# Two-layer hybrid diffusion block: layer 1's modulation weights over GpSimd's queue, the state-space convolutions started earlier, one mLSTM query tile placed in front of a norm

## The chip, the cores and the metric

The kernel runs on one core of one Trainium2 chip. The metric is device time in microseconds of that core, the median of three runs. Below, PE is TensorE, DVE is VectorE, ACT is ScalarE, POOL is GpSimd and SP is SyncE. Nearly all loads are issued on SP's DMA queue.

## The reference, cut to what matters

Two layers run over 256 latent tokens and 256 context tokens of width 1024. The modulation vectors of each layer come from a small product with a wide weight, `w_mod[l]`, of 1024 x 6144; its twelve 512-column chunks are shift, scale and gate of the mixers (chunks 0 to 5) and of the MLP (6 to 11).

```python
for l in range(DEPTH):
    mod_l = silu(c) @ w_mod[l] + b_mod[l]          # and the same with c_ctx for the context
    h = LN(x) * (1 + scale_a) + shift_a            # both streams
    p = split(h @ w_in[l])                         # four mixers:
    a = diff_attention(...)                        # A differential attention
    b = mlstm(silu(dwconv(qk, 5 taps)), ...)       # B
    m = latent_attention(rms_norm(cq) @ w_uq, ...) # C (called mla in the kernel)
    s = ssd(silu(dwconv(xbc, 5 taps)), ...)        # D state space
    y = (sum_k sigmoid(h @ w_gate[k] + b_gate[k]) * (branch_k @ w_branch[k])) @ w_o[l]
    x = LN(alpha * x + gate_a * y)
    u = relu(h2 @ w_up + b_up); x = LN(alpha * x + gate_m * (u * u @ w_down + b_down))
```

In the last layer only the latent stream's output is needed.

## The kernel before, in words

**Products.** Each fp32 product is made of three TensorE products of parts rounded to float32r. `load` (from L154) takes a weight tile of 128 x 1024 (512 KB) over SP's queue into one of four `raw` tiles (L167); ACT writes the high part `whi` (L169), DVE the low part `wlo` (L170), three tiles of each; `three` (L181 to L183) issues the three matmuls. A tile of eight 128 x 128 blocks feeds 24 matmuls.

**Order.** Each engine executes its own list of instructions strictly in the order in which the program's scheduler has put them. The program itself interleaves work by hand: `along(quantum, generator)` starts a side generator that gets one step for every so many microseconds of planned TensorE time of the main line, and `finish` runs what is left of it. `load` takes one step of a list `bg` whenever it is called, as long as the list has any.

**One layer.** `mixers` first makes the mLSTM tile 0 (`mlstm_in`, 24 matmuls a tile in layer 0), the latent attention's compressed queries (`mla_cq`: per token tile a square with a sum on ACT, L1179, a power on POOL, L245, a scaled copy on ACT, L1181, and three transposes on PE, L237 out of `D`), then `mla_in`, and then runs gates and latent attention beside the remaining mLSTM and state-space input tiles. `mlstm_conv` and `ssd_conv` are the five-tap convolutions on DVE (`conv`: L642 four times a tile and L645), six tiles of them for the state space. `merge` makes gated sums of the branches, with the mLSTM, its output and the state-space recurrence running beside it; the mLSTM's own steps on DVE are L678 (a masked bank that PE fills at L660) and L792.

**Modulation of layer 1.** It is computed during layer 0's MLP, chunks 1 and 2 of its four chunks of 1024 hidden units, by 32 `bg` steps. `mod_steps` (chunks 0 to 3) loads four `T` tiles of 128 x 512 on SP's queue (L392) for each of the eight 128-row blocks and multiplies them on PE (L408). `mod_slow` (chunks 4 to 11) loads one `T` tile of 256 KB a step on SP's queue (L434), one ahead within a chunk, and multiplies it on DVE by one column of `ct` (L446 the first, L448 the others: 64 in all). `T` is a pool of eight tiles. `br` is a pool of three larger tiles, two of which hold `x`. In `down`, DVE adds finished banks into `acc` at L1517 and so frees the banks for PE; POOL's queue brings bias rows into `acc` (L1511) and gate rows into `T` (L1485).

Of the kernel before, what the change touches and what calls it, by code (L numbers as in the profile page):

```python
# [10 lines left out]
F32 = mybir.dt.float32  # L11
F32R = mybir.dt.float32r
AF = mybir.ActivationFunctionType
# [5 lines left out]
P = 128  # L19
D = 1024  # L20
KT = D // P
# [38 lines left out]
class Kern:  # L60
# [80 lines left out]
    def step(self, g):  # L141
        try:
            next(g[0])
        except StopIteration:
            self.side.remove(g)
# [231 lines left out]
    def mod_steps(self, l, chunks, bank, tile=None, ahead=False):  # L377

        nc = self.nc
        st = {}  # L380

        def fetch(k):
            raws = []
            for a in range(0, len(chunks), 2):
                if tile is None:
                    raw = self.raw.tile([P, 1024], F32, tag="raw", name="raw")
                    raws += [raw[:, 0:512], raw[:, 512:1024]]
                    nc.sync.dma_start(raw, self.ap["w_mod"][l, k * P:(k + 1) * P, chunks[a] * 512:chunks[a] * 512 + 1024])
                else:
                    for i in range(2):  # L390
                        raws.append(tile())
                        nc.sync.dma_start(raws[-1], self.ap["w_mod"][l, k * P:(k + 1) * P, chunks[a + i] * 512:chunks[a + i] * 512 + 512])  # L392
            st[k] = raws

        def step(k):
            if not ahead:
                fetch(k)
            elif k < KT:
                fetch(k)
                k -= 1  # L400
                if k < 0:
                    return
            else:
                k -= 1
            if k == 0:
                st["ps"] = bank()
            for j in range(len(chunks)):
                nc.tensor.matmul(st["ps"][32 * j:32 * j + 32, :], self.ct[:, k, :], st[k][j],  # L408
                                 start=k == 0, stop=k == KT - 1, tile_position=(0, 32 * j))
            if k == KT - 1 and not ahead:  # L410
                finish()

        def finish():
            n = 32 * len(chunks)
            sb = self.dt_()
            nc.scalar.activation(sb[0:n, :], st["ps"][0:n, :], AF.Copy)
            pt = self.mx()
            for b in range(4):
                self.tr(pt[:, b * P:b * P + n], sb[0:n, b * P:(b + 1) * P])
            for j, ch in enumerate(chunks):  # L420
                self.mod_finish(l, ch, pt.rearrange("p (b r) -> p b r", r=P)[:, :, 32 * j:32 * j + 2], slice(0, 2))

        if ahead:
            return [lambda k=k: step(k) for k in range(KT + 1)] + [finish]
        return [lambda k=k: step(k) for k in range(KT)]

    def mod_slow(self, l, ch, streams):

        nc = self.nc
        acc, ws = {}, {}  # L430

        def fetch(k):
            ws[k] = self.tmp()
            nc.sync.dma_start(ws[k], self.ap["w_mod"][l, k * P:(k + 1) * P, ch * 512:(ch + 1) * 512])  # L434

        def step(k):
            if k == 0:
                fetch(0)
            if k + 1 < KT:
                fetch(k + 1)  # L440
            w = ws.pop(k)
            for s in streams:
                cv = self.ct[:, k, s:s + 1]
                if k == 0:
                    acc[s] = self.tmp()
                    nc.vector.tensor_scalar(acc[s], w, cv, None, op0=ALU.mult)  # L446
                else:
                    nc.vector.scalar_tensor_tensor(acc[s], w, cv, acc[s], op0=ALU.mult, op1=ALU.add)  # L448
            if k == KT - 1:
                pt = self.mx()  # L450
                for s in streams:
                    for b in range(4):
                        o = 8 * s + 2 * b
                        nc.tensor.matmul(pt[:, o:o + 2], acc[s][:, b * P:(b + 1) * P], self.ones, start=True, stop=True)
                for s in streams:
                    self.mod_finish(l, ch, pt[:, 8 * s:8 * s + 8].rearrange("p (b r) -> p b r", r=2)[:, :, 0:1], slice(s, s + 1))

        return [lambda k=k: step(k) for k in range(KT)]

    def mod_finish(self, l, ch, src, s):  # L460
        nc = self.nc
# [941 lines left out]
    def mixers(self, l, js, late):  # L1403
        c = slice(js[0] * P, T)
        res = {}
        lat = l == L - 1
        if not lat:
            for f in self.misc0:
                f()
            self.mlstm_in(l, js, (0,))  # L1410
            self.mla_cq(l, js)
            self.mla_in(l, js)
        else:
            self.mla_cq(l, js)
            self.mlstm_o(l, js)
            late()
            self.mlstm_in(l, js, (0,))
            for f in self.misc(l):
                f()
            self.mlstm_in(l, js, (1,))  # L1420
            self.mla_in(l, js)

        ga = self.along(5.0, self.gates(l))
        mla = self.along(2.4 if not lat else 3.0, self.mla(l, js, res))
        self.mlstm_in(l, js, (1, 2, 3) if not lat else (2, 3))
        self.xbc = []
        for i in range(5):
            self.ssd_in(l, js, i)
        self.finish(ga)
        self.finish(mla)  # L1430
        self.mlstm_conv(l, js)
        self.ssd_in(l, js, 5)
        self.mlstm_v(l, js)

        self.acc = [self.accp.tile([P, 512], F32, tag="acc%d" % m, name="acc") for m in range(KT)]
        self.mg = []
        if not lat:
            mods = self.along(8.5, self.bg_gen(self.mod_steps(0, (4, 5, 6, 7), self.ops, ahead=True)
                                               + self.mod_steps(0, (8, 9, 10, 11), self.ops, ahead=True)))
        sc = self.along(8.0 if not lat else 5.0, self.ssd_conv(l, js))  # L1440
        ml = self.along(3.2 if not lat else 2.6, self.mlstm(l, js))
        self.merge(l, 2, res["C"], c, True)
        self.finish(ml)
        if not lat:
            self.mlstm_o(l, js)
        mo = self.along(3.8, self.mlstm_out(l, js, res))
        self.diff_v(l, js)
        self.finish(mo)

        self.finish(sc)  # L1450
        sd = self.along(3.9 if not lat else 2.6, self.ssd(l, js))
        self.diff_k(l, js)
        self.merge(l, 1, res["B"], c)
        self.finish(sd)
        if not lat:
            self.finish(mods)
        self.ssd_z(l, js)
        so = self.along(3.0, self.ssd_out(l, js, res))
        self.diff_q(l, js)
        self.finish(so)  # L1460

        self.dn = {}
        df = self.along(3.3 if not lat else 3.0, self.diff(l, js[-2:] + js[:-2]))
        self.merge(l, 3, res["D"], c)
        self.finish(df)
# [53 lines left out]
    def layer(self, l, late):  # L1519
        nc = self.nc  # L1520
        streams = [1, 0] if l < L - 1 else [1]
        js = [0, 1, 2, 3] if l < L - 1 else [2, 3]
# [8 lines left out]
        def out_proj(s):  # L1531
            g = self.gate_row(l, 0, s)
            sums = self.residual(self.ap["w_o"][l], self.mg, x, toks(s), g)
            st = self.ln_stats([x(t) for t in toks(s)], toks(s), sums)
            return {t: self.ln_again(x(t), self.ln_affine(x(t), st[t], g1)) for t in toks(s)}
# [5 lines left out]
        for i, s in enumerate(streams):  # L1541
# [4 lines left out]
            st = out_proj(s)  # L1546
# [5 lines left out]
        self.acc = [None] * KT  # L1552

        if l + 1 < L:
            a = self.mod_steps(l + 1, (0, 1, 2, 3), self.mx, self.tmp)
            b = sum((self.mod_slow(l + 1, ch, (1,)) for ch in range(4, 12)), [])
            bg = sum(([*a[i // 4:i // 4 + (i % 4 == 0)], *b[2 * i:2 * i + 2]] for i in range(32)), [])
            n = len(bg)
        for ch in range(3):
            us = []  # L1560
# [12 lines left out]
        for i, s in enumerate(streams):  # L1573
# [9 lines left out]
            st = {}  # L1583
            for t in toks(s):
# [4 lines left out]
                else:  # L1589
                    for i in range(2):  # L1590
                        c = slice(i * 512, (i + 1) * 512)
# [145 lines left out]
```

## Time and profile before

| | |
|---|---|
| median of 3 runs | 1835.34 us (1834.81 to 1838.74) |
| profiled execution | 1835.2 us |
| its span in the profile | 1833.4 us (1.8 us lie around it) |
| PE busy | 1757.4 us, 96% |
| DVE busy | 1195.0 us, 65% |
| ACT busy | 865.7 us, 47% |
| POOL busy | 81.3 us, 4% |
| moved from HBM | 264.75 MB |
| mean granted TensorE clock | 0.982 of full speed |

An engine's share is its busy time over the span of the profiled execution. A line number names the line of the kernel that issued an instruction; `out<-in` names its tiles. In brackets stands how long the engine was idle before an instruction, and the instruction that released it.

### The profile page before, as it was taken

Reading aid. Unit: us, or ns where it says so; the run is one execution under the profiler, and the core shown is the slowest. Engines: PE = TensorE matmul, PEld = TensorE weight load, DVE = VectorE, ACT = ScalarE, POOL = GpSimd, SP = SyncE. Lnnn points to the kernel's source line nnn. Section 1 sums busy time; section 2 is a strip of 40 time slices with the busy share of each in tenths; the row PEclk is TensorE's granted clock in tenths of the full one; section 3 lists DMA queues with packets and bytes.
Section 4 is the critical chain, followed back from the end, with each engine's and each line's share of the span. In section 5 each row is a group of like instructions: output and inputs, shape, how many; then the busy total and the mean of one; then the engine's idle time right before and its main releaser. Section 6 shows DMA issues by size and latency. Waiting matters only on the chain.

```text
span 1833.4 us, 27817 instructions
## 1 busy us (share of the span) xinstructions
PE 1757.4 (96%) x10612; PEld 1489.0 (81%) x10612; DVE 1195.0 (65%) x2324; ACT 865.7 (47%) x1655; POOL 81.3 (4%) x119
## 2 busy tenths in 40 slices
PE   6889999999999999999999999899999999979997
PEld 3777877877887799888777798877989988969996
DVE  4566476355557668885656469867485777676666
ACT  3545354245435545664313246654364555545552
POOL 0100000000000001100000001110000000000000
PEclk9999999999999999999999999899999999989998
DMA  8131244543231256786776656431233353646653
GB/s 326 51 103 41 76 133 138 144 150 127 74 116 64 81 184 187 238 271 210 196 216 219 164 158 205 150 103 55 93 104 93 104 172 115 208 151 194 185 186 100
DMA packets 86981, 269.73 MB, mean 147 GB/s; under 512 B 10368, under 2 KB 11392, under 8 KB 86848
## 3 DMA queue, kind: packets, MB, share of 16 engines
q1 hardware_dynamic: 83056, 256.14, 45.0%
q0 software_dynamic: 3792, 11.82, 2.1%
q8 instruction: 83, 1.36, 0.3%
q14 instruction: 50, 0.41, 0.1%
HBM read 264.75 MB, written 3.17 MB: 146 GB/s over the span
## 4 chain that ended last, share of the span: by engine, by line
PE 84%; DVE 7%; issue 3%; ACT 3%; DMA 2%; POOL 1%; SPq 0%; POOLq 0%; DVEq 0%; ACTq 0%
PE mm L181 18%; PE mm L182 17%; PE mm L183 17%; PE O L181 3%; PE O L183 3%; PE O L182 3%; PE mx L237 3%; PE mx L181 3%; PE mx L183 3%; PE mx L182 3%; DMA T<-w_mod 2%; PE O L1112 2%; DVE wlo L170 1%; PE mx L1145 1%; ACT whi L169 1%
## 5 line engine op out<-in xcount | busy, mean ns | idle before, releaser
L170 DVE TENSOR_TENSOR wlo<-raw,whi 128x1024 fp32r<-128x1024 f32 (+3 forms) x388 | 461.6, 1190 | 329.6 <-ACT whi L169 325.6
L169 ACT ACTIVATE whi<-raw 128x1024 fp32r<-128x1024 f32 (+3 forms) x388 | 400.7, 1033 | 545.1 <-PE mm L182 196.1
L181 PE MATMUL mm<-h,whi 128*128 128x256 f32 (+1 forms) x1216 | 418.4, 344 | 1.1 <-ACT D L1310 1.1
L183 PE MATMUL mm<-h,wlo 128*128 128x256 f32 (+1 forms) x1216 | 408.9, 336 | 1.0 <-DVE wlo L170 1.0
L182 PE MATMUL mm<-h,whi 128*128 128x256 f32 (+1 forms) x1216 | 408.5, 336 | 0.0
L181 PEld LDWEIGHTS mm<-h,whi 128*128 128x128 f32 x1216 | 232.1, 191 | 46.2 <-issue 19.4
L183 PEld LDWEIGHTS mm<-h,wlo 128*128 128x128 f32 x1216 | 231.8, 191 | 25.5 <-DVE wlo L170 1.7
L182 PEld LDWEIGHTS mm<-h,whi 128*128 128x128 f32 x1216 | 232.0, 191 | 22.1 <-issue 1.9
L181 PE MATMUL mm<-whi,L 128*128 128x512 f32 (+1 forms) x344 | 134.0, 390 | 4.9 <-DVE acc L1517 3.5
L183 PE MATMUL mm<-whi,L 128*128 128x512 f32 (+1 forms) x344 | 132.6, 386 | 0.0
L182 PE MATMUL mm<-wlo,L 128*128 128x512 f32 (+1 forms) x344 | 132.6, 386 | 0.0
L245 POOL TENSOR_TENSOR s<-s,mhalf 128x1 f32<-128x1 f32 (+2 forms) x52 | 45.5, 876 | 1263.8 <-DVE s L244 1194.5
L181 PEld LDWEIGHTS mm<-whi,L 128*128 128x128 f32 x344 | 64.9, 189 | 22.9 <-issue 5.2
L183 PEld LDWEIGHTS mm<-whi,L 128*128 128x128 f32 x344 | 65.0, 189 | 13.6
L182 PEld LDWEIGHTS mm<-wlo,L 128*128 128x128 f32 x344 | 65.1, 189 | 12.9
L237 PE MATMUL mx<-kc,T 128*128 128x128 f32 x320 | 52.5, 289 | 23.4 <-DVE T L283 13.8
L1096 ACT ACTIVATE T<-mx,s 128x512 f32<-128x512 f32 (+1 forms) x72 | 44.1, 615 | 64.9 <-DVE s L1094 64.8
L181 PE MATMUL mm<-whi,h 128*128 128x256 f32 x256 | 73.2, 288 | 0.7 <-ACT whi L169 0.5
L182 PE MATMUL mm<-wlo,h 128*128 128x256 f32 x256 | 72.2, 283 | 0.0
L183 PE MATMUL mm<-whi,h 128*128 128x256 f32 x256 | 71.6, 283 | 0.0
L237 PEld LDWEIGHTS mx<-kc,T 128*128 128x128 f32 x320 | 39.6, 147 | 36.6 <-DVE T L283 16.0
L181 PE MATMUL O<-h,whi 128*128 128x256 f32 (+1 forms) x224 | 69.1, 308 | 0.0
(341 smaller groups left out, 3475.7 us busy)
## 6 DMA issues: line engine op xcount, KB each, us to landing
raw<-w_up SPq DMA_DIRECT2D x80, 512.0 KB, 3.7
raw<-w_down SPq DMA_DIRECT2D x80, 512.0 KB, 4.2
raw<-w_gate SPq DMA_DIRECT2D x72, 512.0 KB, 3.6
raw<-w_in_fm SPq DMA_DIRECT2D x52, 512.0 KB, 3.6
T<-w_mod SPq DMA_DIRECT2D x96, 256.0 KB, 3.9
raw<-w_branch SPq DMA_DIRECT2D x36, 512.0 KB, 3.7
raw<-w_mod SPq DMA_DIRECT2D x32, 512.0 KB, 3.7
raw<-w_o SPq DMA_DIRECT2D x24, 512.0 KB, 4.4
```

The costliest lines, as they stand in the source:

```text
L169: nc.scalar.activation(hi[:, :n], raw[:, :n], AF.Copy)
L170: nc.vector.tensor_sub(lo[:, :n], raw[:, :n], hi[:, :n].bitcast(F32))
L181: mm(ps, a[0], b[0], start=first, stop=False)
L182: mm(ps, a[0], b[1], start=False, stop=False)
L183: mm(ps, a[1], b[0], start=False, stop=last)
L237: self.nc.tensor.transpose(out, in_, self.ident[: in_.shape[0], : in_.shape[0]])
L245: nc.gpsimd.tensor_tensor(out, t, self.mhalf[:, 0:1].to_broadcast([P, n]), op=ALU.pow)
L1096: nc.scalar.activation(Pm[:, 0:nk], S[:, 0:nk], AF.Exp, bias=nm, accum_out=ssum)
L1112: self.nc.tensor.matmul(out, aT[:, b * P:(b + 1) * P], v[b][:, h * P:(h + 1) * P], start=b == 0, stop=b == nb - 1)
L1145: nc.tensor.matmul(S[cc][:, 0:nk], self.dq[h][r, c], self.dk[h][r, 0:nk], start=True, stop=True)
```

## The change

Three parts.

1. Layer 1's modulation weights are loaded by POOL's queue. For chunks 0 to 3, `mod_beside` loads one `br` tile of 1 MB for each block of 128 rows (L436 of the changed kernel) and multiplies it one step later (L431). For chunks 4 to 11, `mod_slow` loads its `T` tiles on POOL's queue (L452), two ahead and across the chunks' borders.
2. `ssd_conv` starts right after `mlstm_conv`, with a quantum of 8.0 in layer 0 and 4.0 in layer 1, instead of at the first merge with 8.0 and 5.0.
3. In layer 0, mLSTM tile 1 stands between `mla_cq` and `mla_in`, instead of behind `mla_in` beside the latent attention.

```diff
+    def mod_beside(self, l, chunks):
...
+        def step(k):
+            if k > 0:
+                if k == 1:
+                    st["ps"] = self.mx()
+                for j in range(4):
+                    nc.tensor.matmul(st["ps"][32 * j:32 * j + 32, :], self.ct[:, k - 1, :], st["w"][:, j, :],
+                                     start=k == 1, stop=k == KT, tile_position=(0, 32 * j))
+            if k < KT:
+                st["w"] = self.br(F32)
+                c = chunks[0] * 512
+                nc.gpsimd.dma_start(st["w"], self.ap["w_mod"][l, k * P:(k + 1) * P, c:c + 2048].rearrange("p (a e) -> p a e", a=4))
+            else:
+                self.mod_turn(l, chunks, st["ps"])
...
-    def mod_slow(self, l, ch, streams):
+    def mod_slow(self, l, chunks, streams):
...
-            nc.sync.dma_start(ws[k], self.ap["w_mod"][l, k * P:(k + 1) * P, ch * 512:(ch + 1) * 512])
...
+        units = [(ch, k) for ch in chunks for k in range(KT)]
...
+        def fetch(i):
+            if i < len(units):
+                ch, k = units[i]
+                ws[i] = self.tmp()
+                nc.gpsimd.dma_start(ws[i], self.ap["w_mod"][l, k * P:(k + 1) * P, ch * 512:(ch + 1) * 512])
...
+        def step(i):
+            ch, k = units[i]
+            if i == 0:
                 fetch(0)
...
+                fetch(1)
+            fetch(i + 2)
+            w = ws.pop(i)
...
             self.mla_cq(l, js)
+            self.mlstm_in(l, js, (1,))
             self.mla_in(l, js)
...
-        self.mlstm_in(l, js, (1, 2, 3) if not lat else (2, 3))
+        self.mlstm_in(l, js, (2, 3))
...
         self.mlstm_conv(l, js)
+        sc = self.along(8.0 if not lat else 4.0, self.ssd_conv(l, js))
         self.ssd_in(l, js, 5)
         self.mlstm_v(l, js)
...
-        sc = self.along(8.0 if not lat else 5.0, self.ssd_conv(l, js))
...
-            a = self.mod_steps(l + 1, (0, 1, 2, 3), self.mx, self.tmp)
-            b = sum((self.mod_slow(l + 1, ch, (1,)) for ch in range(4, 12)), [])
-            bg = sum(([*a[i // 4:i // 4 + (i % 4 == 0)], *b[2 * i:2 * i + 2]] for i in range(32)), [])
+            a = self.mod_beside(l + 1, (0, 1, 2, 3))
+            b = self.mod_slow(l + 1, range(4, 12), (1,))
+            at = {round(31 * i / KT): i for i in range(KT + 1)}
+            bg = sum(([*([a[at[i]]] if i in at else []), *b[2 * i:2 * i + 2]] for i in range(32)), [])
```

What the scheduler made of it is seen in the engines' lists, in three places. The first is PE in layer 0, where `mla_cq` ends; its transposes are the L237 out of `D`, and the L181 to L183 into `mm` are the matmuls of mLSTM tile 1:

```order
 L183 MATMUL mx<-whi,h 128x384
-L237 MATMUL mx<-kc,D 128x128 x10
+L181 MATMUL mm<-h,whi 128x512
+L182 MATMUL mm<-h,whi 128x512
+L237 MATMUL mx<-kc,D 128x128 x3
+L183 MATMUL mm<-h,wlo 128x512
+L181 MATMUL mm<-h,whi 128x512
+L182 MATMUL mm<-h,whi 128x512
+L237 MATMUL mx<-kc,D 128x128 x3
...
+L237 MATMUL mx<-kc,D 128x128
 L237 MATMUL mx<-kc,L 128x128 x8
```

Of the 24 matmuls of mLSTM tile 1, 2 now stand ahead of the first group of three transposes, 3 ahead of the second, 6 ahead of the third, 7 ahead of the fourth, and the last 6 behind them. In exchange 24 matmuls are gone from the stretch of the latent attention: between its last scores and their first transposes stand 6 matmuls and 2 attention products now, where 9 matmuls stood.

The second place is DVE's list in layer 1's first merge, beside the mLSTM (L678 of before is L707 of the changed kernel, L1315 is L1344, L768 is L797). Before:

```order
L642 SCALAR_TENSOR_TENSOR D_12701<-L_12016,cols_118,D_12701 128x2x254
L170 TENSOR_TENSOR wlo_12763<-raw_12761,whi_12762 128x1024
L642 SCALAR_TENSOR_TENSOR D_12701<-L_12016,cols_118,D_12701 128x2x255
L678 SCALAR_TENSOR_TENSOR T_12718<-mx_12715,kc_116 128x256
L642 SCALAR_TENSOR_TENSOR D_12701<-L_12016,cols_118,D_12701 128x2x255
L170 TENSOR_TENSOR wlo_12874<-raw_12872,whi_12873 128x1024
L642 SCALAR_TENSOR_TENSOR D_12701<-L_12016,cols_118,D_12701 128x2x254
L678 SCALAR_TENSOR_TENSOR T_12719<-mx_12715,kc_116 128x256
```

After:

```order
L170 TENSOR_TENSOR wlo_12742<-raw_12740,whi_12741 128x1024
L707 SCALAR_TENSOR_TENSOR T_12697<-mx_12694,kc_116 128x256
L707 SCALAR_TENSOR_TENSOR T_12698<-mx_12694,kc_116 128x256
L797 TENSOR_TENSOR T_12697<-T_12705,T_12697 128x256
L1344 SCALAR_TENSOR_TENSOR acc_12486<-D_12724,mm_12726 128x256
L170 TENSOR_TENSOR wlo_12844<-raw_12842,whi_12843 128x1024
```

The convolutions' steps (L642; L671 of the changed kernel) stand here no more: all of them stand further ahead now, between weight tiles of the mLSTM's values and of the first merge's beginning.

The third place is POOL's list in layer 0's MLP. The rows with L436 and L452 were not on this queue; the L1541 are bias rows of `acc`, the L503 and L1515 gate rows:

```order
+L436 DMA br<-w_mod 128x2048
+L1541 DMA acc<-bdown 128x512
 L245 TENSOR_TENSOR s_7263<-s_7264,mhalf 128x1
 L245 TENSOR_TENSOR s_7269<-s_7270,mhalf 128x1
 L245 TENSOR_TENSOR s_7289<-s_7290,mhalf 128x1
 L245 TENSOR_TENSOR s_7309<-s_7310,mhalf 128x1
...
+L452 DMA T<-w_mod 128x512 x44
+L503 DMA gd_557<-modt_115 128x4x1
+L452 DMA T<-w_mod 128x512 x4
+L436 DMA br<-w_mod 128x2048
```

The loads stand behind the powers of the second stream's norm, 44 in a row. On DVE the 64 multiplies move with them: 34 now stand ahead of the first weight tile of the MLP's chunk 1, where 8 stood. From SP's list 80 rows are gone, among them all loads of layer 1's modulation weights.

## Rows read from the trace of the kernel before

**Rows 1.** The page: busy time and share of the engines, and the chain by engine.

```profile
PE 1757.4 (96%) x10612; PEld 1489.0 (81%) x10612; DVE 1195.0 (65%) x2324; ACT 865.7 (47%) x1655; POOL 81.3 (4%) x119
...
PE 84%; DVE 7%; issue 3%; ACT 3%; DMA 2%; POOL 1%; SPq 0%; POOLq 0%; DVEq 0%; ACTq 0%
```

**Rows 2.** Windows: stretch, its length, PE busy (instructions), granted clock, DMA share, GB/s.

```profile
77.70:84.20 6.50, 2.00 (x12) 0.89 0.29 81
84.20:89.70 5.50, 5.46 (x21) 0.51 0.01 3
933.60:938.00 4.40, 1.05 (x9) 1.00 0.67 206
938.00:943.00 5.00, 4.85 (x14) 0.66 0.93 305
1336.00:1338.10 2.10, 0.81 (x4) 1.00 0.39 92
1338.10:1342.40 4.30, 4.30 (x23) 0.60 0.20 80
```

**Rows 3.** Timeline of PE behind the compressed queries: start, length, instruction [idle before, releaser].

```profile
78.59 0.55 PE L237 MATMUL mx<-kc,D 128*128 128x128 f32 x3 [0.54 <-ACT D L1181]
...
81.82 0.55 PE L237 MATMUL mx<-kc,D 128*128 128x128 f32 x3 [1.69 <-ACT D L1181]
84.24 0.47 PE L237 MATMUL mx<-kc,D 128*128 128x128 f32 x1 [1.88 <-ACT D L1181]
```

**Rows 4.** Timeline of PE in layer 0's MLP, columns as in rows 3.

```profile
938.15 0.47 PE L181 MATMUL mm<-whi,L 128*128 128x512 f32 x1 [3.50 <-DVE acc L1517]
...
938.92 0.39 PE L181 MATMUL O<-whi,L 128*128 128x512 f32 x1
939.15 0.40 PE L182 MATMUL O<-wlo,L 128*128 128x512 f32 x1
```

**Rows 5.** Timeline of DVE ahead of it, columns as in rows 3.

```profile
931.47 0.76 DVE L448 SCALAR_TENSOR_TENSOR T<-T,ct 128x512 f32<-128x512 f32 x1 [1.62 <-DMA T<-w_mod]
...
935.52 0.75 DVE L448 SCALAR_TENSOR_TENSOR T<-T,ct 128x512 f32<-128x512 f32 x1 [1.70 <-DMA T<-w_mod]
...
937.32 0.68 DVE L1517 TENSOR_TENSOR acc<-acc,mm 128x512 f32<-128x512 f32 x1
```

**Rows 6.** Waits of SP's queue: total us, times, longest.

```profile
SPq L434 <- DMA T<-w_mod: 46.5, 27, 7.7
```

**Rows 7.** Timelines of DVE and PE in layer 1's first merge, columns as in rows 3.

```profile
1336.18 0.74 DVE L642 SCALAR_TENSOR_TENSOR D<-L,cols,D 128x508 f32<-128x508 f32 x1
...
1337.41 0.36 PE L660 MATMUL mx<-rhl,e 128*128 128x256 f32 x1 [0.98 <-DVE T L678]
1338.07 0.39 PE L181 MATMUL mm<-h,whi 128*128 128x256 f32 x1 [0.30 <-ACT D L1310]
...
1356.54 0.71 PE L781 MATMUL mx<-st,L 64*128 64x129 f32 x4 [0.98 <-DVE T L792]
```

**Rows 8.** Windows: length, busy of PE, PEld, DVE, ACT, POOL, clock, DMA share, GB/s.

```profile
0.00:46.00 46.00, 31.97 (x140) 16.64 (x140) 20.72 (x76) 15.96 (x30) 3.79 (x12) 0.93 0.88 325
166.00:200.00 34.00, 33.80 (x201) 28.64 (x200) 14.21 (x25) 14.15 (x24) 0.00 (x0) 1.00 0.21 63
800.00:828.00 28.00, 28.00 (x171) 24.97 (x171) 24.43 (x36) 15.75 (x25) 0.00 (x0) 1.00 0.89 291
796.00:861.00 65.00, 64.65 (x378) 56.90 (x378) 47.46 (x67) 35.34 (x52) 0.00 (x0) 1.00 0.75 243
1312.00:1334.00 22.00, 22.00 (x203) 20.97 (x202) 15.74 (x29) 10.34 (x19) 0.00 (x0) 1.00 0.30 97
```

**Rows 9.** Timeline of POOL in layer 0's MLP, columns as in rows 3.

```profile
739.36 0.58 POOL L1511 DMA_DIRECT2D acc<-bdown  x1
...
774.92 2.40 POOL L245 TENSOR_TENSOR s<-s,mhalf 128x1 f32<-128x1 f32 x1 [26.18 <-DVE s L244]
```

More of the change, by code (lines that the diff above doesn't have):

```diff
@@ L413, in finish @@
         def finish():
[L414 to L421, printed above, removed]
+            self.mod_turn(l, chunks, st["ps"])
         if ahead:
@@ L425, in mod_steps @@
         return [lambda k=k: step(k) for k in range(KT)]
-    def mod_slow(self, l, ch, streams):
+    def mod_beside(self, l, chunks):
+        nc = self.nc
+        st = {}
+        def step(k):
[10 more added lines that the diff above has]
+            else:
+                self.mod_turn(l, chunks, st["ps"])
+        return [lambda k=k: step(k) for k in range(KT + 1)]
+    def mod_slow(self, l, chunks, streams):
         nc = self.nc
         acc, ws = {}, {}
-        def fetch(k):
-            ws[k] = self.tmp()
-            nc.sync.dma_start(ws[k], self.ap["w_mod"][l, k * P:(k + 1) * P, ch * 512:(ch + 1) * 512])
-        def step(k):
-            if k == 0:
+        units = [(ch, k) for ch in chunks for k in range(KT)]
[7 more added lines that the diff above has]
+            if i == 0:
                 fetch(0)
-            if k + 1 < KT:
-                fetch(k + 1)
-            w = ws.pop(k)
+                fetch(1)
+            fetch(i + 2)
+            w = ws.pop(i)
             for s in streams:
@@ L456, in step, with mod_turn @@
                     self.mod_finish(l, ch, pt[:, 8 * s:8 * s + 8].rearrange("p (b r) -> p b r", r=2)[:, :, 0:1], slice(s, s + 1))
-        return [lambda k=k: step(k) for k in range(KT)]
+        return [lambda i=i: step(i) for i in range(len(units))]
+    def mod_turn(self, l, chunks, ps):
+        n = 32 * len(chunks)
+        sb = self.dt_()
+        self.nc.scalar.activation(sb[0:n, :], ps[0:n, :], AF.Copy)
+        pt = self.mx()
+        for b in range(4):
+            self.tr(pt[:, b * P:b * P + n], sb[0:n, b * P:(b + 1) * P])
+        for j, ch in enumerate(chunks):
+            self.mod_finish(l, ch, pt.rearrange("p (b r) -> p b r", r=P)[:, :, 32 * j:32 * j + 2], slice(0, 2))
     def mod_finish(self, l, ch, src, s):
```

## The prediction

> **What bounds the kernel now.** I read the page first: PE is busy for 1757.4 of 1833.4 us and holds 84% of the chain that ended last, DVE 7% [rows 1]. So PE is the bound, and the change adds and removes nearly no matmuls. What can be won is PE's idle time, 1833.4 − 1757.4 = 76 us in all, and busy time in which PE's granted clock is low. Then I listed PE's waits and looked for those that stand where the diff touches the order; the windows around each give PE's busy time and the clock. There are three such places, and the reader should see the same pattern in each [rows 2]: a stretch in which PE waits (2.00 us busy of 6.50, 1.05 of 4.40, 0.81 of 2.10), and behind it a stretch in which PE is busy at a clock of 0.51, 0.66 and 0.60 of full speed, between its levels 2.4 and 1.2 GHz. The wait is paid twice.
>
> **Place A, mLSTM tile 1 in front of the norm (layer 0, 78 to 90 us).** The transposes of the compressed queries wait for ACT's scaled copies, with 0.54, 1.69 and 1.88 us of idle time in three of four groups [rows 3]; the chain is ACT, DVE, POOL and ACT again, a token tile at a time, and it does not get shorter. The change puts 18 of the tile's 24 matmuls between these groups. A 512-column matmul takes 0.23 us at full clock (938.92 to 939.15, [rows 4]), so 18 × 0.23 = 4.1 us of work is done while the chain runs, and the group at 84.24 starts when it did. These 4.1 us are then missing later. PE's busy time in the 6.5 us becomes 2.0 + 4.1 = 6.1, so I expect no fall of the clock behind it. That stretch held 5.46 us of work at 0.51 [rows 2]; at full clock it would take 5.46 × 0.51 = 2.8, which is 2.7 less; I take 2.5, since parts of it start by the chain's pace. A gives 6.6. Bounds: 4.1 (the clock falls all the same) and 6.8. The tile's own weight parts cost nothing: their ACT and DVE instructions stand ahead of the chain in the order, where both engines idle.
>
> **Place D, what the tile leaves behind (layer 0, up to 178 us).** In the latent attention the tile's 24 matmuls were cover for softmax. PE lost 0.2 us of 34 in 166 to 200 [rows 8], so there is no wait now. With less cover the whole row of products ends earlier, and between the last scores and their transposes stand 6 matmuls (1.4 us) and two attention products instead of 9 (2.1 us). So at the last few tiles perhaps 0.4 us each comes uncovered: about 1.1 in all for three. Bounds: 0, and 5.5 if all the cover was needed (24 × 0.23). I take 1.1, since the previous stretch has no wait at all.
>
> **Place B, modulation loads off SP (layer 0's MLP, 931 to 943 us).** PE waits 3.50 us for DVE's addition into acc [rows 4], which frees the bank. DVE is late because multiplies of `mod_slow` ahead of it on DVE wait for their `T` tile, 1.62 and 1.70 us at 931.47 and 935.52; the addition comes at 937.32 [rows 5]. The tile is late since its load sits on SP's queue, one ahead only, and the queue itself stood 46.5 us waiting for such tiles [rows 6]. After the change the loads stand on POOL's queue, which has little else, two ahead; and more than half of the multiplies are over before. The wait goes: 3.5 us. The stretch behind it had 4.85 us of work at 0.66 [rows 2], so up to 4.85 × 0.34 = 1.6 comes back, of which I take 1.5. B gives 5.0. Bounds 3.5 and 5.1.
>
> **Place F, where these multiplies go (796 to 861 us).** 34 multiplies instead of 8 now stand on DVE ahead of chunk 1's first weight tile. One takes 0.75 us [rows 5], so 26 × 0.75 = 19.5 us come to the 47.46 us that DVE is busy there in 65 [rows 8]: 67 us. DVE becomes the bound of this stretch by 2 us. The transfers become tight as well: 243 GB/s × 65 us = 15.8 MB; 15 loads of layer 1's modulation go from it (8 for DVE, 7 for PE, 0.26 MB each), 34 come: 20.8 MB. At 325 GB/s, the highest that a window shows, this takes 64 us, and at 291 GB/s, which 800 to 828 had at a share of 0.89, 71.5 us [rows 8]. Two weight tiles that are ready ahead can take up some of it. I take a cost of 3, near DVE's excess plus a little for the transfers. Bounds: 0, and 8 (71.5 − 65 plus something for the excess). Behind it, DVE is freer by the same 19.5 us, but PE has no wait there other than place B.
>
> **The loads' queue.** A load issued by POOL held it for 0.58 us [rows 9], so 34 take 20 us of the 65, and no power or bias row that PE needs soon stands behind them in the order; cost 0. The eight 1 MB tiles have about 22 us of PE work between them, and a tile of that size at 243 GB/s takes 4.3 us; cost 0.
>
> The Trainium skill speaks against this part of the change: by "SBUF — State Buffer" (section "SBUF: two separate sides"), a DMA from GpSimd's queue has its descriptors written by GpSimd, which is locked out while VectorE runs in a mode with two ports, and it advises the SP or ACT queue. Its figure is about 620 ns alone against 3100 ns beside a copy on VectorE; by that, as an estimate, 34 loads would take 105 us instead of 21 and the sum would be some 40 us higher. The trace has the 0.58 us beside a DVE that was busy in most of that time, and agrees with the first figure; no run here shows the second.
>
> **Place C, the convolutions (layer 1, 1336 to 1357 us).** PE waits 0.98 for L678 and 0.30 behind that; DVE had a convolution step of 0.74 us at 1336.18 directly ahead of this L678, and one of the same length ahead of the L792 for which PE waits 0.98 at 1356.54 [rows 7]. After the change no convolution stands there. I count 1.28, 0.7 of the second wait, and the clock: 4.30 us at 0.60 [rows 2] give up to 4.30 × 0.40 = 1.7, of which 1.5. C gives 3.5. Bounds 1.3 and 3.7. What moves ahead, 16 steps of 0.74 = 11.8 us with the closing ones on top, falls into about 1288 to 1330; in 1312 to 1334 DVE was busy for 15.74 of 22 [rows 8], part of which is these same steps, and PE did not wait at all. Cost 0, with 3 as the bound where one step meets a weight tile at the wrong moment several times. In layer 0 the convolutions go from a stretch without waits to 166 to 200, where DVE is busy for 14.21 of 34 [rows 8]: neither gain nor cost.
>
> **The sum**, from the profiled execution's 1835.2 (which is the median, 1835.34, within 0.2): −6.6 (A) − 5.0 (B) − 3.5 (C) + 1.1 (D) + 3.0 (F) = −11.0, so **1824.2 us**.
>
> **Rivals.**
> 1. *The tile was needed as cover* (place D at its bound): 5.5 instead of 1.1, so 1828.6. Against it: PE has no waits there, and 6 matmuls remain between.
> 2. *Stretch F becomes bound by DVE and transfers*: 8 instead of 3, so 1829.2; with the clock falling there too, some 1831. For it: 67 of 65 us on DVE and a rate at the highest seen. Against it: tiles ready ahead, and the multiplies can slip between the `wlo` only if these are late.
> 3. *POOL's queue issues too slowly* (the slower side). One power on POOL took 2.40 us [rows 9]. If a load took that beside a busy DVE, 34 loads would need 82 us in a stretch of 65: the weight tiles of chunk 1 stand behind multiplies that wait, PE loses 17 us, and the time is 1824.2 + 17 = 1841. It decides from 65/34 = 1.9 us a load. Against it: 0.58 [rows 9]. It is the form that the rule quoted above would take here.
> 4. *The waits stay*: the banks in B or the masked bank in C are late for another reason, or the clock stays low. With the lower bounds of A, B and C, 1835.2 − 8.9 + 4.1 = 1830.4. That the change does not do what it says is excluded by the order: the matmuls, loads and steps did move.
>
> **Chances.** The forecast (1819 to 1828) 0.58; rival 1 0.09; rival 2 0.15; rival 3 0.06; rival 4 0.12. About 0.2%, 3.7 us, is what a measurement of this kernel can tell from no change: faster is below 1831.6, slower above 1839. All of the forecast and rival 1, and most of rivals 2 and 4, lie in faster: 0.79. Rival 2 with more lost and rival 4 with D or F at its bound lie within: 0.13. Rival 3, and F and D at their bounds together (1835.2 − 8.9 + 13.5 = 1839.8), are slower: 0.08. The range: all gains at their upper bounds without any cost would give 1835.2 − 15.6 = 1819.6, and it reaches up to where rivals 1, 2 and most of 4 end: 1818 to 1833.
>
> **What would show it.** A: the transposes behind the compressed queries with idle time below 1.3 us together, and a clock near 1 in the 6 us behind. B: no wait of PE for the addition into acc near the end of chunk 2, no load of `w_mod` for layer 1 on SP. C: no idle time of PE ahead of L689 (the old L660) in the first merge, and a clock of 1. D: idle time of PE of some tenths ahead of the last transposes of the latent attention. F: DVE near 100% and 290 to 325 GB/s in the 65 us ahead of chunk 1, with PE waits on `wlo` of about 3 us. The prediction is wrong if PE waits more than 8 us in F, if POOL's DMA issues take over 1.9 us, or if the attention's softmax now ends the waits for over 5 us.

## The result, and the profile after

The changed kernel takes 1825.74 us (median of 6 runs, 1824.92 to 1829.35) against 1836.81 for the kernel before in the same session (6 runs, 1834.81 to 1838.74): a ratio of 0.9943, with a 95% interval of 0.993 to 0.9955. The prediction was 1824.2, range 1818 to 1833. The profiled span goes from 1833.4 to 1824.4 us; that is 9.0 us where the medians differ by 11.1, since the profiled execution of before (1835.2) was shorter than its median.

The page of the changed kernel, busy time and share of the engines, and the chain that ended last, as in [rows 1]:

```profile
PE 1751.1 (96%) x10612; PEld 1482.2 (81%) x10612; DVE 1196.8 (66%) x2324; ACT 866.6 (48%) x1655; POOL 119.2 (7%) x191
...
PE 82%; DVE 7%; issue 5%; ACT 3%; POOL 2%; DMA 1%; SPq 0%; POOLq 0%; ACTq 0%; DVEq 0%
```

POOL has 38 us more: 72 more DMA issues of about half a microsecond. PE has as many matmuls as before and 6.3 us less busy time; the low clock at the places below is the part of it that can be pointed at.

To see where 9.0 us went I walked both traces along PE: each matmul counts as work of the spacing that its shape usually has, and at equal work I took the difference of the two times. Where A ends and D begins, the tile's 24 matmuls lie on different sides of the line in the two kernels, so this walk can't part A from D; A is taken by two instructions instead that both kernels have (the rows under A). The parts of the difference, after minus before, by the places of the prediction:

| stretch | difference, us | forecast |
|---|---|---|
| up to the compressed queries | −0.4 | 0 |
| A: compressed queries and the norm | −4.7 | −6.6 |
| D: attention and its tail | −1.0 | +1.1 |
| the rest of layer 0's mixers, first part of its MLP | +0.2 | 0 |
| F: ahead of chunk 1 | +4.7 | +3.0 |
| B: chunks 1 and 2 up to the old wait | −4.5 | −5.0 |
| from there to layer 1's first merge | +0.1 | 0 |
| C: layer 1's first merge | −4.3 | −3.5 |
| all behind it | +1.0 | 0 |
| sum | −9.0 | −11.0 |

**A.** Windows of PE in the changed kernel (length, PE busy, clock, DMA share, GB/s), to be held against the first two of [rows 2]:

```profile
77.20:83.80 6.60, 6.03 (x30) 1.00 0.12 32
83.80:89.30 5.50, 4.06 (x24) 1.00 0.09 21
```

and its waits of PE from 76 to 93 us (total, times, longest):

```profile
PE mm L181 <- ACT L L1238: 1.4, 1, 1.4
PE mm L181 <- ACT L L1260: 1.0, 1, 1.0
PE mx L237 <- ACT D L1210: 0.5, 2, 0.3
```

PE is busy for 6.03 of 6.60 us where it was for 2.00 of 6.50, the transposes wait for 0.5 us in place of the idle times in [rows 3], and the clock stays at 1.00 where it was 0.51. What this is worth is read from PE's first and last common instruction of the stretch, before and after:

```profile
77.72 0.34 PE L183 MATMUL mx<-whi,h 128*128 128x384 f32 x1
92.43 0.39 PE L181 MATMUL mm<-whi,L 128*128 128x256 f32 x1 [1.01 <-ACT L L1231]
```

```profile
77.29 0.33 PE L183 MATMUL mx<-whi,h 128*128 128x384 f32 x1
83.81 0.33 PE L237 MATMUL mx<-kc,D 128*128 128x128 f32 x1 [0.25 <-ACT D L1210]
92.83 0.39 PE L181 MATMUL mm<-whi,L 128*128 128x256 f32 x1 [1.01 <-ACT L L1260]
```

The way from the first to the last is 14.71 us before and 15.54 after, and the second holds the tile's 24 matmuls more, 24 × 0.23 = 5.5 us of work: A is −4.7. The fourth group of transposes comes 6.52 us behind the first row in both kernels (84.24, in [rows 3], less 77.72; 83.81 less 77.29), so the 18 matmuls ahead of it, 4.1 us, are all gained. Behind it only 0.6 us is.

In the list of waits the first line is new: PE waits 1.4 us for ACT's scaled copy L1238. ACT's timeline shows what stands ahead of it:

```profile
86.43 0.63 ACT L169 ACTIVATE whi<-raw 128x512 fp32r<-128x512 f32 x1
...
87.22 0.59 ACT L718 ACTIVATE L<-mm 128x512 f32<-128x512 f32 x1
87.69 0.69 ACT L1238 ACTIVATE L<-mx,cols 128x512 fp32r<-128x512 f32 x1
```

L718 is the copy of the mLSTM tile's own result. The tile was put in front of the norm with its copy, and that copy now stands ahead of the copy that the next products need. It holds ACT for 0.47 us (87.22 to 87.69). The weight part ahead of it holds ACT for about as long, and it comes late too: in the kernel before, the third weight part of this stretch stands among the transposes.

```profile
78.44 0.62 ACT L169 ACTIVATE whi<-raw 128x512 fp32r<-128x512 f32 x1
```

I take it that the tile's own weights hold one of the three `whi` tiles until its last matmul. Both are a part of the 1.4 us; no run takes either away.

**F and B.** Windows of all engines (columns as in [rows 8]) and PE's clock behind the wait:

```profile
796.00:861.00 65.00, 62.07 (x353) 53.93 (x352) 58.12 (x86) 30.70 (x42) 16.16 (x31) 0.97 0.91 308
```

```profile
845.30:848.30 3.00, 0.41 (x2) 1.00 0.69 232
848.30:853.20 4.90, 4.90 (x15) 0.65 0.88 285
```

The timelines of DVE and PE at the same place:

```profile
844.44 0.75 DVE L467 SCALAR_TENSOR_TENSOR T<-T,ct 128x512 f32<-128x512 f32 x1 [2.15 <-DMA T<-w_mod]
845.76 0.75 DVE L467 SCALAR_TENSOR_TENSOR T<-T,ct 128x512 f32<-128x512 f32 x1 [0.57 <-DMA T<-w_mod]
...
847.57 0.68 DVE L1547 TENSOR_TENSOR acc<-acc,mm 128x512 f32<-128x512 f32 x1
...
848.30 0.50 PE L181 MATMUL mm<-whi,L 128*128 128x512 f32 x1 [2.59 <-DVE acc L1547]
```

This is the picture of [rows 4] and [rows 5] at another place: a multiply waits for its tile, the addition that frees the bank stands behind it, PE waits, and the clock falls behind that. What the change removes near 934 us it makes anew at 845. DVE was busy for 58.12 of 65 us, not for all of it, and it waits for transfers while 308 GB/s flow. POOL's load of the tile for which the multiply at 844.44 waits:

```profile
838.34 0.54 POOL L452 DMA_DIRECT2D T<-w_mod  x1 [2.93 <-DVE T L467]
```

It was issued when a multiply had freed its buffer, and the tile came some 6 us later; the median from issue to landing of the `T` loads of `w_mod` was 3.9 us in the kernel before and is 4.8 in this one. Near 932 us 0.5 us of the old 3.5 is left.

**C.** PE in layer 1's first merge:

```profile
1320.00:1350.00 30.00, 30.00 (x247) 1.00 0.34 112
```

No idle time and no low clock are left of [rows 7] and of the last two of [rows 2]. One wait is new, just ahead of this window:

```profile
1317.64 0.48 DVE L671 SCALAR_TENSOR_TENSOR D<-L,cols,D 128x254 f32<-128x254 f32 x1
...
1318.21 0.42 ACT L673 ACTIVATE D<-D 128x256 f32<-128x256 f32 x1 [0.67 <-DVE D L671]
1318.54 0.46 ACT L1339 ACTIVATE D<-mm,hb 128x256 f32<-128x256 f32 x1
...
1319.05 0.38 PE L181 MATMUL mm<-h,whi 128*128 128x256 f32 x1 [1.05 <-ACT D L1339]
```

The convolutions' own ACT step (L673) waits for their step on DVE and stands ahead of the copy (L1339) for which PE waits. The kernels without the moved convolutions have no wait of PE between 1290 and 1330 us.

### The profile page after: what moved, and what is told of

The parts are those of the page before. It is cut to its first block, busy times and chain, and to the rows that moved or that the text cites. A ratio compares the mean times of both kernels' runs of the same rounds, so it can differ in the third digit from the quotient of the medians.

```text
span 1824.4 us, 27827 instructions
## 1 busy us (share of the span) xinstructions
PE 1751.1 (96%) x10612; PEld 1482.2 (81%) x10612; DVE 1196.8 (66%) x2324; ACT 866.6 (48%) x1655; POOL 119.2 (7%) x191
## 4 chain that ended last, share of the span: by engine, by line
PE 82%; DVE 7%; issue 5%; ACT 3%; POOL 2%; DMA 1%; SPq 0%; POOLq 0%; ACTq 0%; DVEq 0%
PE mm L181 17%; PE mm L183 16%; PE mm L182 16%; PE mx L181 3%; PE mx L183 3%; PE mx L182 3%; PE O L181 3%; PE O L182 3%; PE O L183 3%; PE mx L237 3%; PE O L1141 2%; DVE wlo L170 1%; PE mx L1174 1%; PE O L408 1%; PE mm L408 1%
## 5 line engine op out<-in xcount | busy, mean ns | idle before, releaser
L169 ACT ACTIVATE whi<-raw 128x1024 fp32r<-128x1024 f32 (+3 forms) x388 | 400.7, 1033 | 524.3 <-PE mm L182 193.9
L181 PE MATMUL mm<-h,whi 128*128 128x256 f32 (+1 forms) x1216 | 417.3, 343 | 1.6 <-ACT D L1339 1.6
L183 PE MATMUL mm<-h,wlo 128*128 128x256 f32 (+1 forms) x1216 | 409.0, 336 | 1.0 <-DVE wlo L170 1.0
L181 PEld LDWEIGHTS mm<-h,whi 128*128 128x128 f32 x1216 | 231.4, 190 | 46.9 <-issue 19.5
L183 PEld LDWEIGHTS mm<-h,wlo 128*128 128x128 f32 x1216 | 231.1, 190 | 25.5 <-DVE wlo L170 1.9
L181 PE MATMUL mm<-whi,L 128*128 128x512 f32 (+1 forms) x344 | 134.2, 391 | 4.9 <-DVE acc L1547 3.5
L183 PE MATMUL mm<-whi,L 128*128 128x512 f32 (+1 forms) x344 | 133.1, 387 | 0.0
L181 PEld LDWEIGHTS mm<-whi,L 128*128 128x128 f32 x344 | 65.1, 190 | 23.7 <-DVE acc L1547 3.8
L183 PEld LDWEIGHTS mm<-whi,L 128*128 128x128 f32 x344 | 65.2, 189 | 13.7
L237 PE MATMUL mx<-kc,T 128*128 128x128 f32 x320 | 52.8, 290 | 23.5 <-DVE T L283 13.8
L181 PE MATMUL mm<-whi,h 128*128 128x256 f32 x256 | 73.1, 288 | 0.6 <-ACT whi L169 0.5
L183 PE MATMUL mm<-whi,h 128*128 128x256 f32 x256 | 71.5, 283 | 0.0
L237 PEld LDWEIGHTS mx<-kc,T 128*128 128x128 f32 x320 | 39.6, 148 | 36.7 <-DVE T L283 15.8
L181 PE MATMUL O<-h,whi 128*128 128x256 f32 (+1 forms) x224 | 69.1, 309 | 0.0
```

Of the source, the lines that this page charges most:

```text
L169: nc.scalar.activation(hi[:, :n], raw[:, :n], AF.Copy)
L181: mm(ps, a[0], b[0], start=first, stop=False)
L183: mm(ps, a[1], b[0], start=False, stop=last)
L237: self.nc.tensor.transpose(out, in_, self.ident[: in_.shape[0], : in_.shape[0]])
```

## The experiments

The theory after the result: three places gain, and the loads and multiplies of `mod_slow`, drawn together ahead of chunk 1, lose there what their removal from chunk 2 gains, because the transfers can't keep up. The rivals: GpSimd's queue is the cause of the loss; VectorE's busy time is; or the gain belongs to one part only.

**Each part alone**, on the kernel before. The mLSTM tile:

```diff
             self.mla_cq(l, js)
+            self.mlstm_in(l, js, (1,))
             self.mla_in(l, js)
...
-        self.mlstm_in(l, js, (1, 2, 3) if not lat else (2, 3))
+        self.mlstm_in(l, js, (2, 3))
```

> The third part alone: mLSTM tile 1 in front of the norm in layer 0. Theory: minus 5.8 us, of it 4.1 from matmuls in the chain's gaps and the rest from the clock behind them, less 0.2 in the attention's tail: 1829.5 within 1 us. Rival (the tail of the attention needs the tile as cover once the convolutions are not there to be moved with it): minus 3 us or less, 1832 and above.

Measured: 1831.86 us against 1835.79, ratio 0.9976 (0.9967 to 0.9985). Its A is −4.7 us, as in the changed kernel, and its whole profiled difference −4.6. The theory's 1829.5 within 1 is missed, and the time is near the rival's 1832, whose reason (a tail without cover) does not show: the waits of the tail are those of before. The longer times go with a lower mean granted clock: four of the eleven runs took 1830.4 to 1830.7 us at 0.985 or 0.986, seven 1831.5 to 1835.5 at 0.983. One place where the clock can fall or stay up is seen under D below.

The convolutions:

```diff
         self.mlstm_conv(l, js)
+        sc = self.along(8.0 if not lat else 4.0, self.ssd_conv(l, js))
...
-        sc = self.along(8.0 if not lat else 5.0, self.ssd_conv(l, js))
```

> The second part alone: the state-space convolutions from the latent attention's end on. Theory: the gain lies in layer 1's first merge alone, minus 4.3 us, so 1831 within 1 us, and layer 0 as before. Rival (in layer 0 the convolutions now meet the attention's tail, or weight tiles of the first merge come late in layer 1): 1833 to 1836.

Measured: 1833.75 us, ratio 0.9987 (0.9978 to 0.9995), so 0.9 to 4.0 us where the theory had some 4.3 and 1831; the theory's number is missed. C is −4.3 as in the changed kernel, and layer 0 shows nothing at the place where they went; but the profiled execution has no gain in all, since its old wait in chunk 2 was longer than that of before:

```profile
PE mm L181 <- DVE acc L1517: 5.4, 1, 5.4
```

In the profile of before it was 3.5 [rows 4], in that of the tile alone 4.4. The old wait differs by some us between these profiled executions, and with it, I take it, the times of all kernels that still have it (1833.4 to 1839.4 in 27 runs of the kernel before).

The modulation weights (the first part of the diff, with the other two lines as before):

> The first part alone: layer 1's modulation weights by GpSimd's queue, the other two parts left as before. Theory: the wait for the addition into acc near the end of the MLP's chunk 2 and the low clock behind it go (minus 4.5 us), and the 34 multiplies and loads that are drawn into the 65 us ahead of chunk 1 give about the same back (plus 4.5): 1835 within 2 us, with a wait of PE for the addition into acc of 2 to 3 us at the end of chunk 0's second stream. Rival (this part is the change's gain, and the loss ahead of chunk 1 comes from the parts together): 1830 to 1831.

Measured: 1834.58 us, ratio 0.9989 (0.9981 to 0.9998); F is +4.3 and B −3.2, as expected. This part alone is worth 0.4 to 3.5 us by its interval, 1.2 by the medians: it gives in one place most of what it takes in the other. The three ratios add up to −0.11 − 0.13 − 0.24 = −0.48%, the change has −0.57% (0.45 to 0.70), so nothing shows that the parts help or hinder each other.

**Is it the bunching?** The changed kernel, with the multiplies held back until the program has come to them:

```diff
+                if k == 0:
+                    gt[s] = self.small(KT)
+                    nc.vector.scalar_tensor_tensor(gt[s], self.last[:, 0:KT].bitcast(F32), 0.0, self.ct[:, :, s],
+                                                   op0=ALU.mult, op1=ALU.add)
-                cv = self.ct[:, k, s:s + 1]
+                cv = gt[s][:, k:k + 1]
```

`self.last` is the low part that `load` made last; the copy adds zero times its values.

> The changed kernel, but each group of eight multiplies on VectorE reads its column of the conditioning from a small copy that is written only after the last weight tile in the program's order, so the multiplies can't run ahead of chunk 1 (5 of the 64 in front of it instead of 34) and are spread over chunks 1 and 2; the loads stay on GpSimd's queue. Theory (the loss is that too many multiplies and loads are bunched into the stage ahead of chunk 1): 4 to 5 us below the changed kernel, 1821 to 1822, no PE wait for the addition into acc ahead of chunk 1. Rival (GpSimd's queue delivers the tiles late, wherever they stand): the wait moves to chunk 1 or 2 and the time is that of the changed kernel, 1825 to 1827.

Measured: 1820.12 us (1819.93 to 1821.66, 4 runs), ratio 0.9911 (0.9897 to 0.9925). F is −0.3, B −5.1. PE's only wait from 790 to 960 us is one for the norm that was there before:

```profile
PE mx L238 <- DVE T L284: 0.5, 1, 0.5
```

Three multiplies now stand ahead of chunk 1 where 34 stood. So the theory holds, and this kernel is faster than both: 5.6 us under the changed one (medians of two sessions; 0.32% by the ratios). The rival, late tiles by GpSimd's queue wherever they stand, is refuted, since the queue is the same.

**Transfers or VectorE?** First, all multiplies, but one load for each eight (seven of eight weight tiles are left out, so layer 1's modulation is not that of the reference):

```diff
+                if i % KT:
+                    ws[i] = ws[i - i % KT]
+                    return
                 ws[i] = self.tmp()
```

> The changed kernel with only 8 of the 64 tiles of chunks 4 to 11 loaded: each group's multiplies all read the group's first tile, so layer 1's modulation is computed from wrong weights; the multiplies and their places on VectorE stay. It takes 14.7 MB away from the transfers, most of it ahead of and in chunk 1. Theory (the loss ahead of chunk 1 is a wait of the multiplies for transfers at a rate near the highest): the loss of 4.7 us goes to under 1, the time 1820 to 1822. Rival (VectorE's own busy time, 67 of 65 us, is the loss): 3 us or more stay, 1824 to 1826.

Measured: 1820.73 us, ratio 0.9918 (0.9904 to 0.9933), F +0.1. Its window (columns as in [rows 8]):

```profile
796.00:861.00 65.00, 64.92 (x373) 56.67 (x372) 64.19 (x95) 31.21 (x43) 1.07 (x2) 1.00 0.64 195
```

DVE is busy for 64.19 of 65 us, and PE loses nothing. So DVE's load, by which I had sized the loss, is not the cause. The loads are; whether by the rate alone, or also because a load can only be issued when one of the eight `T` tiles is free, this run does not tell, and a larger pool was not tried.

Second, all loads, but seven of eight multiplies on 32 of 512 columns (the modulation is incomplete):

```diff
-                    nc.vector.scalar_tensor_tensor(acc[s], w, cv, acc[s], op0=ALU.mult, op1=ALU.add)
+                    nc.vector.scalar_tensor_tensor(acc[s][:, 0:32], w[:, 0:32], cv, acc[s][:, 0:32], op0=ALU.mult, op1=ALU.add)
```

> The changed kernel with all 64 tiles loaded, but seven of each eight multiplies done on 32 of the 512 columns, so layer 1's modulation is incomplete; VectorE is freed of some 0.6 us for each, the transfers stay. Theory (transfers): the multiplies still wait for tiles that are drawn ahead of chunk 1 at the same rate, but VectorE has time to catch up: 1 to 3 us of the 4.7 stay, 1822 to 1825. Rival (VectorE's busy time alone): all of it goes, 1820 to 1821.

Measured: 1835.04 us, as slow as before (0.9999, 0.9988 to 1.001). Both expectations missed, and in the direction that the theory of transfers should have told: cheaper multiplies free their tiles sooner, so more loads are drawn ahead, 40 instead of 34 multiplies stand before chunk 1, and F is +12.3. Window and waits of PE, 796 to 861 us, and DVE ahead of the longest of them, which ends at 852.20:

```profile
796.00:861.00 65.00, 56.22 (x320) 47.90 (x319) 43.24 (x89) 28.88 (x44) 20.49 (x38) 0.97 0.91 314
```

```profile
PE mm L182 <- DVE wlo L170: 4.6, 2, 2.9
PE mm L183 <- DVE wlo L170: 1.8, 3, 0.9
PE O L183 <- DVE wlo L170: 1.4, 2, 0.8
PE mm L181 <- DVE acc L1547: 1.0, 2, 0.6
```

```profile
849.31 0.25 DVE L467 SCALAR_TENSOR_TENSOR T<-T,ct 128x32 f32<-128x32 f32 x1 [2.27 <-DMA T<-w_mod]
850.76 0.25 DVE L467 SCALAR_TENSOR_TENSOR T<-T,ct 128x32 f32<-128x32 f32 x1 [1.20 <-DMA T<-w_mod]
850.93 1.22 DVE L170 TENSOR_TENSOR wlo<-raw,whi 128x1024 fp32r<-128x1024 f32 x1
```

PE waits for `wlo`, with DVE busy for only 43 of 65 us. The weight tiles themselves are not what is late: by the profile no instruction of the window waits for a `raw` tile's transfer. `wlo` is late because it stands behind multiplies that wait for their `T` tiles, at 314 GB/s: the picture of the changed kernel, with `wlo` in the place of the addition. With VectorE relieved and the loads kept, the loss is larger, so the transfers of the `T` tiles, and not VectorE's work, hold this stretch. That full multiplies held the loads back fits, but was not tried by itself.

**Which queue?** The 64 tiles on SP's queue, in the changed kernel and in the paced one:

```diff
-                nc.gpsimd.dma_start(ws[i], self.ap["w_mod"][l, k * P:(k + 1) * P, ch * 512:(ch + 1) * 512])
+                nc.sync.dma_start(ws[i], self.ap["w_mod"][l, k * P:(k + 1) * P, ch * 512:(ch + 1) * 512])
```

> The changed kernel with the 64 tiles of chunks 4 to 11 loaded by SP's queue again, still two ahead and across the chunks' borders; their multiplies stand on VectorE nearly where the changed kernel has them, 34 to 37 ahead of chunk 1. Theory (bunching, not the queue, costs the time ahead of chunk 1): the loss there stays, 3 us or more, the time 1825 to 1828, within 0.2% of the changed kernel. Rival (GpSimd's queue is what makes the tiles late there): the loss goes, 1821 to 1822.

Measured: 1825.24 us (1824.51 to 1826.36), ratio 0.994 (0.9926 to 0.9955): the changed kernel's time. F is +2.7, a bit under the 3 that I expected to stay, with one wait of 2.6 us; 30 multiplies stand ahead of chunk 1, not 34 to 37. F is 2.0 less than in the changed kernel's profile, and that the times are equal all the same has D in it, which is about 1.2 more here (under D below): one profiled execution each can't tell whether the queue is worth a microsecond or two in F.

> The paced kernel (1820.1) with the same 64 tiles on SP's queue. It tells whether the wait near the end of chunk 2 was taken away by the queue or by loading two ahead. Theory (in SP's list a tile's load stands behind weight loads that wait for a free tile, so it comes late and VectorE waits for it): 2 to 5 us slower than the paced kernel, 1822 to 1825, with waits of VectorE for these tiles of over 1 us each. Rival (two ahead is enough on either queue): 1820 within 1 us.

Measured: 1821.28 us (1820.61 to 1823.66), ratio 0.9917 (0.9901 to 0.9934), the same as the paced kernel's 0.9911 within the intervals; F −0.4, B −5.1, and PE has no wait in chunks 1 and 2. The theory of this run (SP's queue brings them late) falls, and the rival's 1820 within 1 is missed by 0.3; VectorE does wait for tiles, up to 4.2 us, but nothing that PE needs stands behind. On which queue the loads stand shows in the time of neither kernel.

**What cured the old wait, then?** Under the paced multiplies on SP's queue, the old habits back one at a time: one tile ahead within a chunk instead of two across them, and four `T` tiles a step for chunks 0 to 3 instead of one `br` tile.

```diff
-            if i == 0:
-                fetch(0)
-                fetch(1)
-            fetch(i + 2)
+            if k == 0:
+                fetch(i)
+            if k + 1 < KT:
+                fetch(i + 1)
```

> The paced kernel with the 64 tiles on SP's queue (1821.3), now loaded one ahead within a chunk, as before the change; chunks 0 to 3 stay with the 1 MB tile. It tells what cured the wait near the end of chunk 2. Theory (the second tile ahead did it): the wait of PE for the addition into acc is back once or more with 2 to 5 us, the time 1823 to 1827. Rival (the four tiles a step of the old way for chunks 0 to 3 crowded the pool of eight): no such wait, 1820 to 1822.

```diff
-            a = self.mod_beside(l + 1, (0, 1, 2, 3))
+            a = self.mod_steps(l + 1, (0, 1, 2, 3), self.mx, self.tmp)
...
-            at = {round(31 * i / KT): i for i in range(KT + 1)}
+            at = {4 * i: i for i in range(KT)}
```

> Two tiles ahead on SP's queue, paced, and chunks 0 to 3 loaded as before the change, four tiles of the pool of eight a step. Theory (the second tile ahead is the cure): no wait, 1820 to 1822. Rival (crowding of the pool): the wait of 2 to 5 us is back, 1823 to 1827.

And both together:

> As the run with one tile ahead on SP's queue, and chunks 0 to 3 are loaded as before the change too, four tiles of the pool of eight a step; so all of the old loading is back, under paced multiplies. Both theories: the wait for the addition into acc is back with 3 to 5 us and a low clock behind it, the time 1824 to 1828. A third possibility, that the pacing alone cures it: 1820 to 1822.

Measured, with PE's wait for the addition into acc from 850 to 1060 us: one ahead 1823.06 us (0.9925, 0.9908 to 0.9941), a wait of 0.5 us; four `T` tiles 1820.90 (0.9914, 0.99 to 0.9929), none; both 1826.48 (0.9943, 0.9928 to 0.9957), and the wait is back:

```profile
PE mm L182 <- DVE acc L1552: 3.2, 1, 3.2
```

So in the paced kernel either cure is nearly enough by itself, the loading two ahead and across chunks entirely; the wait needs both old habits. Neither of my two theories alone says that: one tile ahead gave the theory's time (1823 to 1827) without its wait of 2 to 5 us.

## Why the prediction was right, point by point

The time, 1825.74, lies 1.5 us above the forecast and the sign is right. That it lies so near is in part luck: A gave 1.9 less than forecast and F cost 1.7 more, and this is made up by 2.1 in D, from a clock that happened to stay up, and 0.8 in C. The forecast also counted from 1835.2, and the kernel before had a median of 1836.81 beside the changed one. By steps:

**A** was forecast as −6.6 and is −4.7, also in every other kernel with the tile moved. The 18 matmuls in the gaps came as worked out, 4.1 us, and the clock stayed up. But the 2.5 us that the clock was to give became 0.6: where PE crept at 0.51 before, it is now done sooner and waits for ACT. The sentence that the tile's own weight parts cost nothing failed, and it left out the copy of the result: a weight part (L169) and that copy (L718) now stand on ACT ahead of L1238, for which PE waits 1.4 us.

**D** was forecast as +1.1 and is −1.0. Windows of PE up to the end of the attention's long wait and behind it, of the changed kernel, of before, and of the run with the tiles on SP's queue:

```profile
132.20:137.20 5.00, 1.66 (x9) 1.00 0.17 46
137.20:142.20 5.00, 5.00 (x30) 1.00 0.21 66
```

```profile
131.80:136.80 5.00, 1.65 (x9) 1.00 0.19 47
136.80:141.80 5.00, 5.00 (x19) 0.66 0.14 58
```

```profile
133.20:138.20 5.00, 1.66 (x9) 1.00 0.22 52
138.20:143.20 5.00, 5.00 (x19) 0.66 0.14 56
```

The wait did not change, 2.6 us in all three, but the clock behind it stayed up in the changed kernel. Among the ten profiled kernels that have the tile in front of the norm, four kept the clock and have a D of −0.6 to −1.1, the six others −0.1 to +0.4. So the clock is worth about 1.1 us here, and the missing cover 0.4 at most: the idle time that the prediction expected ahead of the last transposes did not appear (33.92 of 34 us busy in 166 to 200), and PE's waits from 100 to 225 us are those of before within 0.1 each. A and D together are worth −5.8 to −4.3, and the tile alone measured −2.8 to −6.1 by its interval, −3.9 by the medians.

**F** was forecast as +3 and is +4.7. Here a step failed and not only a size: I took DVE's excess over the 65 us and a little for the transfers. DVE was not the limit (64.19 of 65 us, and no wait of PE, with one load in eight); the transfers were. The forecast's own figure from 20.8 MB at 291 GB/s, +6.5, misses by as much on the other side (1.8), but it names what binds; the changed kernel moved 308 GB/s × 65 us = 20.0 MB there. The sign to look for, waits on `wlo` of about 3 us, had the wrong form too: PE waits 2.6 and 0.3 us for the addition into `acc`.

**B** was forecast as −5.0 and is −4.5, or −5.1 where all of the wait is gone. The chain (tile, multiply, addition, bank, PE, clock) was right. The reason given for its cure was not: with SP's queue the wait is gone as well, paced or not. In the paced kernels two tiles ahead, or fewer tiles of the pool taken by chunks 0 to 3, are what helps; in the changed kernel itself that was not taken apart.

**The queue** itself cost nothing, as forecast: 31 instructions took 16.16 us of POOL in the 65 us, 0.52 each, beside a DVE that was busy for 58. The two figures of the Trainium skill ("SBUF — State Buffer", section "SBUF: two separate sides") with which the prediction reckoned, about 620 and 3100 ns, are times of a DMA and not of its issue. POOL's 0.52 us a load can be set beside the lower one only as the prediction did, and no run here shows the higher one. The advice of the Trainium skill in the same section, to use the SP or ACT queue, makes no difference to the time in the two pairs that try SP's (1825.74 and 1825.24; 1820.12 and 1821.28).

**C** was forecast as −3.5 and is −4.3: the 0.98 us wait for L792 went entirely, and so did the low clock. But the low clock does not come in every execution. In the two kernels where nothing was changed there (the tile alone, the modulation weights alone) the same waits stand and the stretch is 1.5 us shorter than in the profile of before; PE behind the first of them, with the modulation weights alone:

```profile
1339.00:1343.00 4.00, 3.88 (x31) 1.00 0.23 92
```

The clock is 1.00 where [rows 2] have 0.60. So about 2.8 of the 4.3 is the change, which is nearer to what the convolutions alone gave (2.0 by the medians, 0.9 to 4.0). The new wait of 1.05 us at 1319 is in it; the prediction had put what moves ahead at nothing, with 3 as its bound.

**Rivals.** Rival 2 is what happened in part, by its transfers. Rival 1 costs 0.4 at most, rival 3 did not occur, and of rival 4 only that the clock's share in A was not gained.

## What to carry to other kernels

Work that is moved off a late queue goes where the scheduler finds room, not where it was meant to stand: count where it lands, and whether the transfers of that stage can carry it. A load with a large lead needs something that holds it back; here one small copy that depends on the current weight tile is worth 5.6 us, more than the modulation weights' part alone (1.2). Where a wait is in front of the bottleneck engine, price it with the low clock behind it, but look whether another wait takes the place of the slow stretch, whether the clock falls there in every execution, and what the filler itself puts on the engine that the next step waits for.

## What the runs showed of the hardware

The same wait is followed by different clocks. In the thirteen profiled kernels the attention's wait is 2.6 us, with PE busy for 1.6 to 1.7 of the five microseconds up to its end in those shown above; behind it nine have a clock of 0.66 to 0.73 of full speed over five microseconds, and four have 1.00. The 0.98 us wait in layer 1's first merge has 0.60 behind it in the profile of before and 1.00 in two kernels with the same waits. What decides it stays open; it is worth 1.1 to 1.5 us a time and makes profiles of one execution uncertain by as much.

DVE can be busy for 99% of 65 us without PE noticing: 64.19 us with PE busy for 64.92, in the run with one load for each eight. Transfers gave way earlier: at 308 GB/s over 65 us a multiply waited 2.15 us for its tile, and at 314 another waited 2.27, with the weight part that PE needed behind it.
